# The first two tiles of an input projection in halves of the tokens

## The chip, the cores and the metric

The kernel runs on one core of one Trainium2 chip. The metric is the time of one execution in microseconds (us), measured on the device. The kernel before takes 2940.47 us, the median of three runs (2937.76 to 2942.84).

## The reference, cut to what matters

The reference is one hybrid decoder block over 512 tokens of 2048 channels in float32: an RWKV-7 time mixer and a sliding-window attention side by side, merged by sigmoid gates, then a gated feed-forward with a short convolution. What the change touches is its first step:

```python
h = rms_norm(x, norm1_g[l])      # per token: x * rsqrt(mean(x^2) + eps) * g
z = h @ w_in[l]                  # 2048 channels in, all branches' inputs out
...
q = za[..., :ATT_Q_DIM]
k = za[..., ATT_Q_DIM:ATT_Q_DIM + ATT_KV_DIM]
v = za[..., ATT_Q_DIM + ATT_KV_DIM:]
```

Each row (token) of `x` is scaled by a number of its own and each channel by its gain; the result is multiplied by the columns of `w_in`.

## The kernel before

**Products in three parts.** Every operand of a large product is split into a high part (the value rounded to the matmul format fp32r) and a low part (the rest). A product is three matmuls: high by high, high by low, low by high. Three such matmuls for one block of 128 channels are called one step here; a tile of 128 output columns takes 16 steps, 48 matmuls of 512 columns (the tokens), into one PSUM bank.

**The start.** `x` arrives in four tiles `xt[t]` of 128 tokens (line 171). ScalarE squares and sums each tile (L293), VectorE makes the reciprocal root of two tiles' sums in `rsqrt_small` (L188 to L197, thirteen small operations) and scales the two tiles (L296). That is done for the first two tiles (tokens 0 to 255, half `h=0`), then for the other two (`h=1`). Then, per half and per block `k` of 128 channels, TensorE transposes the two 128x128 pieces into a PSUM tile `ps_x` (L303), ScalarE writes the high part `xhi` with the gain (L305), and VectorE the low part `xlo` (L306). That is 2 x 16 columns, each 256 tokens wide, through six PSUM buffers.

**The weights.** `load_w` (L236) fetches four blocks of a tile's weights (256 KB) by a DMA on the queue of SyncE (SP) into one of four `raw` buffers, ScalarE writes the high part `whi` (L243), VectorE the low part `wlo` (L244), in three buffers each. `project` (L250) calls it four times a tile and issues the matmuls (L258 to L260). The first three loads of the first tile are written ahead of the columns, as `first`.

**The order of the tiles.** 72 tiles: the keys' first tile (`c_ka`), the values' first (`c_va`), further keys and values, queries, the RWKV inputs, the gates. `ztile` (L313) gives a tile an accumulator of the pool `accA` (three banks). Behind a tile of keys `qk_norm` takes sums of squares on TensorE (`head_stats`, L333) and turns them by a transpose (L336).

**Sums of weights in DRAM.** The later stages need sums of blocks of `w_out` and `w_down`. They are made in DRAM beside the projection: every third call of `load_w` (every fourth in the last 28 loads, `wp["step"] = 4`) starts one job, a DRAM to DRAM copy of 512 KB on SP (L227) and an accumulating DMA on GpSimd's queue (POOL, L228). Further jobs follow in the stages behind the projection. There are 120 in all.

**What sets the order.** The kernel is written in a framework that sets semaphores and orders each engine's instructions itself. An instruction passed through `pin` keeps its place relative to the other pinned instructions of its engine; the rest may be moved. Each engine works through its own list in order. In the projection before, the start and the loads of weights are not pinned.

**Towards the end of the projection** the outputs of the two branches are fetched from DRAM by DMAs on POOL's queue (`rin`, `ain`, L780 and L782), while the last gate tiles run.

Of the kernel before, what the change touches and what calls it, by code (L numbers as in the profile page):

```python
# [20 lines left out]
NT = S // P  # L21
# [5 lines left out]
RMS_EPS = 1e-6  # L27
# [107 lines left out]
def block_kernel(ctx: ExitStack, tc: tile.TileContext, d: Dims, a: dict, out: bass.AP):  # L135
    nc = tc.nc
    act, dve, pool, pe, sync = nc.scalar, nc.vector, nc.gpsimd, nc.tensor, nc.sync
    NK, NP, NQ, NKV, NF = d.NK, d.NP, d.NQ, d.NKV, d.NF
# [16 lines left out]
    ident = const.tile([P, P], F32, name="ident")  # L155
# [5 lines left out]
    cst = cstp.tile([P, NCONST - P], F32, name="cst")  # L161
# [18 lines left out]
    def col(nm, i=0):  # L180
        return pcol[:, PR[nm] + i : PR[nm] + i + 1]
# [51 lines left out]
        wp["raw"] = stack.enter_context(tc.tile_pool(name="wraw", bufs=nraw, side=side, reuse_waits="tile"))  # L233
        wp["hl"] = stack.enter_context(tc.tile_pool(name="whl", bufs=nhl, side=side, reuse_waits="tile"))

    def load_w(src):  # L236
        nk, ncol = src.shape[1:]
        n = nk * ncol
        raw = wp["raw"].tile([P, 512], F32, name="raw", tag="raw")[:, :n].rearrange("p (k c) -> p k c", c=ncol)
        wp["last"] = sync.dma_start(raw, src)  # L240
        hi = wp["hl"].tile([P, 512], F32R, name="whi", tag="whi")[:, :n].rearrange("p (k c) -> p k c", c=ncol)
        lo = wp["hl"].tile([P, 512], F32R, name="wlo", tag="wlo")[:, :n].rearrange("p (k c) -> p k c", c=ncol)
        act.activation(hi, raw, AF.Copy)  # L243
        dve.tensor_tensor(lo, raw, hi.bitcast(F32), op=ALU.subtract)  # L244
        wp["n"] += 1
        if wp["n"] % wp["step"] == 0:
            sums_along()()
        return hi, lo

    def project(acc, src, xhi, xlo, pre=()):  # L250
        nk = src.shape[1]
        for k0 in range(0, nk, 4):
            n = min(4, nk - k0)
            whi, wlo = pre[k0 // 4] if k0 // 4 < len(pre) else load_w(src[:, k0 : k0 + n])
            for j in range(n):
                k = k0 + j
                first, last = k == 0, k == nk - 1
                pe.matmul(acc, whi[:, j], xhi[:, k], start=first, stop=False)  # L258
                pe.matmul(acc, whi[:, j], xlo[:, k], start=False, stop=False)  # L259
                pe.matmul(acc, wlo[:, j], xhi[:, k], start=False, stop=last)  # L260
# [20 lines left out]
    pa = ExitStack()  # L281
    open_weights(pa, 4, 3, "right")
    if True:
        xhi = by_k(big(big1, "xhi", "h1"))
        xlo = by_k(big(big1, "xlo", "l1"))
        zt = {c: a["w_z"][i].rearrange("p (k c) -> p k c", c=P) for i, c in enumerate(d.z_tiles())}
        with tc.tile_pool(name="x0_ps", bufs=6, space=PSUM) as ps0:
            ssum = p0.tile([P, NT], F32, name="ssum")
            HT = NT // 2
            for h in range(2):  # L290
                for t in range(h * HT, (h + 1) * HT):
                    sq = p0.tile([P, d.D], F32, name="sqx", tag="sqx", bufs=1)
                    act.activation(sq, xt[t], AF.Square, accum_out=ssum[:, t : t + 1])  # L293
                r = rsqrt_small(p0, ssum[:, h * HT : (h + 1) * HT], 1.0 / d.D, RMS_EPS)
                for t in range(HT):
                    dve.tensor_scalar(xt[h * HT + t], xt[h * HT + t], r[:, t : t + 1], None, op0=ALU.mult)  # L296
            first = {d.c_ka: [load_w(zt[d.c_ka][:, k0 : k0 + 4]) for k0 in range(0, min(NK, 12), 4)]}
            for h in range(2):
                hs = slice(h * HT * P, (h + 1) * HT * P)
                for k in range(NK):  # L300
                    ps = ps0.tile([P, HT * P], F32, name="ps_x", tag="x")
                    for t in range(HT):
                        pe.transpose(ps[:, t * P : (t + 1) * P], xt[h * HT + t][:, k * P : (k + 1) * P], ident)  # L303
                    g = col("n1g", k)
                    act.activation(xhi[:, k, hs], ps, AF.Identity, scale=g)  # L305
                    dve.scalar_tensor_tensor(xlo[:, k, hs], ps, g, xhi[:, k, hs].bitcast(F32), op0=ALU.mult, op1=ALU.subtract)  # L306
        xin.close()
        act.activation(bor, K["bo"], AF.Copy)
        act.activation(cenr, K["cen"], AF.Copy)

        accp = pa.enter_context(tc.tile_pool(name="accA", bufs=3, space=PSUM, side="right", reuse_waits="tile"))
# [464 lines left out]
        with tc.tile_pool(name="ain", bufs=1, side="right", reuse_waits="tile") as ainp:  # L776
# [586 lines left out]
```

## Time and profile before

| | us |
|---|---|
| median of three runs | 2940.47 |
| lowest and highest | 2937.76, 2942.84 |
| the profiled execution, its own time | 2943.37 |
| its span in the trace | 2941.6 |
| TensorE busy | 2895.2 |
| VectorE busy | 1951.8 |
| ScalarE busy | 1315.9 |

The profile is one execution, 2.90 us above the median, and its span is 1.77 us short of its own time. PE is TensorE's matmul row, PEld its loading of the stationary operand (beside matmuls), DVE VectorE, ACT ScalarE, SPq the issuing of SyncE. A row of the timeline has start, duration, engine, line, operation, output and inputs, shapes, count (equal neighbours are merged), and in brackets the idle time before it and what ended that. A row of a table by windows has the window, its length, each engine's busy time with the number of instructions, the clock that was granted to TensorE (1.00 is full), the share of the 16 DMA engines and what they moved in GB/s. Matmuls overlap, so the distance between two starts is the price of one, not its duration.

### The profile page before, as it was taken

How to read it: one execution, taken by the hardware profiler on the slowest of the kernel's cores; microseconds unless marked ns; L12 is line 12 of the kernel's file. 1: busy time of each engine (PE TensorE's matmuls, PEld its weight loads, DVE VectorE, ACT ScalarE, POOL GpSimd, SP SyncE). 2: the span in 40 equal slices, each digit the busy share in tenths (PEclk: the TensorE clock that was granted, in tenths of full speed). 3: DMA queues.
4: the chain of work that ended last, by engine and by line, in shares of the span. 5: the costliest groups of instructions: out<-in, count | busy, mean ns of one | idle time of the engine just before them, and what ended most of it. 6: DMA issues, size and time to landing. Idle time of an engine off the chain costs nothing.

```text
span 2941.6 us, 48281 instructions
## 1 busy us (share of the span) xinstructions
PE 2895.2 (98%) x18826; PEld 2470.2 (84%) x18826; DVE 1951.8 (66%) x3243; ACT 1315.9 (45%) x2133; POOL 218.9 (7%) x286
## 2 busy tenths in 40 slices
PE   7999999999999999999999899999999999999999
PEld 5777777777777777788888899999999999888887
DVE  4555666666666666445567777777777777665555
ACT  4344434334334334332356455455555555544444
POOL 0001000000000000101000001101101110000000
PEclk9999999999999999999999899999999999999999
DMA  7855756656656656877877789888888888877775
GB/s 209 222 150 140 191 128 163 159 130 164 160 131 162 158 126 158 255 234 237 287 249 236 190 234 240 237 226 226 229 235 241 233 229 230 303 239 244 256 258 189
DMA packets 225141, 609.45 MB, mean 207 GB/s; under 512 B 24768, under 2 KB 44944, under 8 KB 223888
## 3 DMA queue, kind: packets, MB, share of 16 engines
q1 hardware_dynamic: 157504, 434.92, 46.6%
q0 software_dynamic: 36064, 132.14, 23.6%
q10 hardware_dynamic: 31344, 39.31, 3.9%
q8 instruction: 147, 2.41, 0.3%
q14 instruction: 82, 0.67, 0.1%
HBM read 556.62 MB, written 174.43 MB: 249 GB/s over the span
## 4 chain that ended last, share of the span: by engine, by line
PE 93%; DVE 2%; ACT 2%; DMA 1%; issue 1%; ACTq 0%; SPq 0%; DVEq 0%; POOLq 0%
PE X L1064 16%; PE acc L260 11%; PE acc L259 11%; PE X L931 11%; PE acc L258 11%; PE Y L931 8%; PE Y L1064 8%; PE Z L1064 4%; PE bulk L644 1%; PE mi L460 1%; PE psG L713 1%; PE bulk L706 1%; PE psS L724 1%; PE bulk L552 1%; PE bulk L683 1%
## 5 line engine op out<-in xcount | busy, mean ns | idle before, releaser
L260 PE MATMUL acc<-xhi,wlo 128*128 128x512 f32 x1152 | 472.2, 410 | 0.0
L258 PE MATMUL acc<-xhi,whi 128*128 128x512 f32 x1152 | 466.1, 405 | 1.9 <-DVE xlo L306 1.9
L259 PE MATMUL acc<-xlo,whi 128*128 128x512 f32 x1152 | 466.2, 405 | 0.0
L243 ACT ACTIVATE whi<-raw 128x512 fp32r<-128x512 f32 x352 | 220.4, 629 | 457.2 <-PE acc L259 372.4
L924 DVE TENSOR_TENSOR wlo<-raw,whi 128x1024 fp32r<-128x1024 f32 x210 | 257.0, 1224 | 207.9 <-ACT whi L923 207.9
L244 DVE TENSOR_TENSOR wlo<-raw,whi 128x512 fp32r<-128x512 f32 x352 | 240.5, 688 | 226.5 <-ACT whi L243 217.7
L923 ACT ACTIVATE whi<-raw 128x1024 fp32r<-128x1024 f32 x210 | 222.6, 1060 | 291.9 <-PE X L931 157.7
L1064 PE MATMUL X<-b,whi 128*128 128x256 f32 x1472 | 271.0, 285 | 2.3 <-DVE u L1084 0.9
L1064 PE MATMUL X<-t,whi 128*128 128x256 f32 x1408 | 260.4, 285 | 8.7 <-DVE u L1084 8.3
L1047 DVE TENSOR_TENSOR wlo<-raw,whi 128x1024 fp32r<-128x1024 f32 x176 | 214.9, 1222 | 78.4 <-ACT whi L1046 77.7
L1064 PE MATMUL Y<-t,whi 128*128 128x256 f32 x1408 | 257.6, 283 | 0.0
L260 PEld LDWEIGHTS acc<-xhi,wlo 128*128 128x128 f32 x1152 | 217.3, 189 | 43.8 <-issue 3.1
L259 PEld LDWEIGHTS acc<-xlo,whi 128*128 128x128 f32 x1152 | 217.4, 189 | 41.7 <-issue 2.2
L258 PEld LDWEIGHTS acc<-xhi,whi 128*128 128x128 f32 x1152 | 217.5, 189 | 41.4 <-issue 2.2
L1046 ACT ACTIVATE whi<-a 128x1024 fp32r<-128x1024 f32 x132 | 139.3, 1056 | 213.7 <-DVE a L1040 211.5
L1064 PEld LDWEIGHTS X<-b,whi 128*128 128x128 f32 x1472 | 231.2, 193 | 3.1 <-issue 2.4
L1064 PEld LDWEIGHTS X<-t,whi 128*128 128x128 f32 x1408 | 222.1, 194 | 9.3 <-DVE u L1084 5.7
L1064 PEld LDWEIGHTS Y<-t,whi 128*128 128x128 f32 x1408 | 220.2, 192 | 0.0
L1064 PE MATMUL X<-b,wlo 128*128 128x256 f32 x736 | 209.5, 285 | 2.1 <-DVE wlo L1047 2.1
L1047 DVE TENSOR_TENSOR wlo<-a,whi 128x1024 fp32r<-128x1024 f32 x132 | 161.7, 1225 | 67.6 <-ACT whi L1046 67.0
L1064 PE MATMUL X<-t,wlo 128*128 128x256 f32 x704 | 200.7, 285 | 0.2
L1064 PE MATMUL Y<-t,wlo 128*128 128x256 f32 x704 | 199.4, 283 | 0.0
(339 smaller groups left out, 6050.0 us busy)
## 6 DMA issues: line engine op xcount, KB each, us to landing
raw<-in_w_up_dram SPq DMA_DIRECT2D x180, 512.0 KB
raw<-in_w_z_dram SPq DMA_DIRECT2D x288, 256.0 KB
s_dn<-in_w_dn_dram POOLq DMA_DIRECT2D x88, 512.0 KB, 6.9
raw<-in_w_up_dram POOLq DMA_DIRECT2D x88, 512.0 KB, 8.3
raw<-s_dn SPq DMA_DIRECT2D x88, 512.0 KB
raw<-in_w_dn_dram SPq DMA_DIRECT2D x66, 512.0 KB
a<-in_w_up_dram SPq DMA_DIRECT2D x48, 512.0 KB
s_dn<-in_w_dn_dram SPq DMA_DIRECT2D x44, 512.0 KB
```

The source lines that it names most:

```text
L243: act.activation(hi, raw, AF.Copy)
L244: dve.tensor_tensor(lo, raw, hi.bitcast(F32), op=ALU.subtract)
L258: pe.matmul(acc, whi[:, j], xhi[:, k], start=first, stop=False)
L259: pe.matmul(acc, whi[:, j], xlo[:, k], start=False, stop=False)
L260: pe.matmul(acc, wlo[:, j], xhi[:, k], start=False, stop=last)
L460: pe.matmul(ps[:, h], pT[:, kb, h], vt[:, n - 1 + kb, g * HD : (g + 1) * HD], start=kb == kbs[0], stop=kb == kbs[-1])
L923: act.activation(whi, wr, AF.Copy)
L924: dve.tensor_tensor(wlo, wr, whi.bitcast(F32), op=ALU.subtract)
L931: pe.matmul(dst, l[:, q, ts], r[:, es], start=fst and j == 0, stop=lst and j == 2, skip_group_check=True)
L1046: pin(act.activation(hi, t, AF.Copy))
L1047: pin(dve.tensor_tensor(lo, t, hi.bitcast(F32), op=ALU.subtract))
L1064: pin(pe.matmul(ps, l[:, k], r[:, k], start=start and k + i == 0, stop=last and i == 2, skip_group_check=True))
```

## The change

The normalised rows are still made in two halves of 256 tokens, in this order now, almost all of it pinned:

- Squares of all four tiles; scale and scaling of the first half; its 16 columns (`columns(0, k)`). The second half's scale is written after the eighth column. After columns 9, 11, 13 and 15 stand the four loads of the first tile's weights, into buffers of their own in the pool of the rows (eight pairs for two tiles).
- Scaling of the second half: one tile on VectorE, one on ScalarE. The DMAs of the constants and of the attention sinks come here on SP instead of at the very start.
- The first tile's products with the first half of the tokens: 48 matmuls of 256 columns.
- For each `k`: at every fourth `k` a load of the second tile's weights; the column `k` of the second half; the second tile's three matmuls of block `k` with the first half.
- The second half of the tokens for the first tile, then for the second: 96 matmuls of 256 columns.

The accumulators of the two tiles are taken ahead of the columns' PSUM buffers, which are five now instead of six. The eight loads of these two tiles do not count towards the sums in DRAM, and the step of four for the last loads is gone, so that it stays three.

```diff
-    def load_w(src):
+    def load_w(src, pl=None, bufs=None, pin=free):
...
-        act.activation(hi, raw, AF.Copy)
-        dve.tensor_tensor(lo, raw, hi.bitcast(F32), op=ALU.subtract)
+        hi, lo = ((pl or wp["hl"]).tile([P, 512], F32R, name=nm, tag=nm, bufs=bufs)[:, :n].rearrange("p (k c) -> p k c", c=ncol)
+                  for nm in ("whi", "wlo"))
+        pin(act.activation(hi, raw, AF.Copy))
+        pin(dve.tensor_tensor(lo, raw, hi.bitcast(F32), op=ALU.subtract))
+        if pl:
+            return hi, lo
         wp["n"] += 1
         if wp["n"] % wp["step"] == 0:
             sums_along()()
...
-    sync.dma_start(sinkb, a["attn_sinks"].rearrange("(o h) -> o h", o=1).to_broadcast([P, d.HQ]))
-    sync.dma_start(cst, a["cst"][:, P:])
...
+        heads = [accp.tile([P, S], F32, name="acc", tag="acc") for _ in range(2)]
+        first = dict(zip((d.c_ka, d.c_va), heads))
+        with tc.tile_pool(name="x0_ps", bufs=5, space=PSUM) as ps0:
...
+            def scales(h):
+                return rsqrt_small(p0, ssum[:, h * HT : (h + 1) * HT], 1.0 / d.D, RMS_EPS)
+
+            def scaled(h, t, r, eng):
+                x = xt[h * HT + t]
+                if eng is dve:
+                    pin(dve.tensor_scalar(x, x, r[:, t : t + 1], None, op0=ALU.mult))
+                else:
+                    pin(act.activation(x, x, AF.Copy, scale=r[:, t : t + 1]))
+
+            def columns(h, k):
...
+                    pin(pe.transpose(ps[:, t * P : (t + 1) * P], xt[h * HT + t][:, k * P : (k + 1) * P], ident))
+                g = col("n1g", k)
+                pin(act.activation(xhi[:, k, hs], ps, AF.Identity, scale=g))
+                pin(dve.scalar_tensor_tensor(xlo[:, k, hs], ps, g, xhi[:, k, hs].bitcast(F32), op0=ALU.mult, op1=ALU.subtract))
+
+            def weights(i, k):
+                ws[i].append(load_w(zt[(d.c_ka, d.c_va)[i]][:, k : k + 4], p0, 2 * NK // 4, pin))
+
+            def half_mm(i, h, k):
+                hs = slice(h * HT * P, (h + 1) * HT * P)
+                whi, wlo = (w[:, k % 4] for w in ws[i][k // 4])
+                for j, (l, r) in enumerate(((whi, xhi), (whi, xlo), (wlo, xhi))):
+                    pin(pe.matmul(heads[i][:, hs], l, r[:, k, hs], start=h == 0 and k + j == 0,
+                                  stop=k == NK - 1 and j == 2, skip_group_check=True))
+
+            r = scales(0)
+            for t in range(HT):
+                scaled(0, t, r, dve)
+            ws = [[], []]
+            for k in range(NK):
+                columns(0, k)
+                if k == NK // 2 - 1:
+                    r = scales(1)
+                if k >= NK // 2 and k % 2:
+                    weights(0, 2 * (k - NK // 2 - 1))
+            for t in range(HT):
+                scaled(1, t, r, act if t else dve)
+            sync.dma_start(cst, a["cst"][:, P:])
+            sync.dma_start(sinkb, a["attn_sinks"].rearrange("(o h) -> o h", o=1).to_broadcast([P, d.HQ]))
+            for k in range(NK):
+                half_mm(0, 0, k)
+            for k in range(NK):
+                if k % 4 == 0:
+                    weights(1, k)
+                columns(1, k)
+                half_mm(1, 0, k)
+            for i in range(2):
                 for k in range(NK):
...
+                    half_mm(i, 1, k)
         xin.close()
-        act.activation(bor, K["bo"], AF.Copy)
-        act.activation(cenr, K["cen"], AF.Copy)
...
+        pin(act.activation(bor, K["bo"], AF.Copy))
+        pin(act.activation(cenr, K["cen"], AF.Copy))
 
         def ztile(c0):
+            if c0 in first:
+                return first.pop(c0)
             acc = accp.tile([P, S], F32, name="acc", tag="acc")
-            project(acc, zt[c0], xhi, xlo, first.pop(c0, ()))
+            project(acc, zt[c0], xhi, xlo)
             return acc
...
-            wp["step"] = 4
```

More of the change, by code (lines that the diff above doesn't have):

```diff
@@ L248, in load_w, with project @@
         return hi, lo
-    def project(acc, src, xhi, xlo, pre=()):
+    def project(acc, src, xhi, xlo):
         nk = src.shape[1]
@@ L253, in project @@
             n = min(4, nk - k0)
-            whi, wlo = pre[k0 // 4] if k0 // 4 < len(pre) else load_w(src[:, k0 : k0 + n])
+            whi, wlo = load_w(src[:, k0 : k0 + n])
             for j in range(n):
@@ L289, in block_kernel @@
             HT = NT // 2
[L290 to L294, printed above, removed]
-                for t in range(HT):
-                    dve.tensor_scalar(xt[h * HT + t], xt[h * HT + t], r[:, t : t + 1], None, op0=ALU.mult)
@@ L297, in block_kernel @@
-            first = {d.c_ka: [load_w(zt[d.c_ka][:, k0 : k0 + 4]) for k0 in range(0, min(NK, 12), 4)]}
-            for h in range(2):
-                hs = slice(h * HT * P, (h + 1) * HT * P)
-                for k in range(NK):
[L301 to L306, printed above, removed]
+            for t in range(NT):
+                sq = p0.tile([P, d.D], F32, name="sqx", tag="sqx", bufs=1)
+                act.activation(sq, xt[t], AF.Square, accum_out=ssum[:, t : t + 1])
```

6 lines of the change are left out of this document (2 added, 4 removed).

## The prediction

> **What bounds the kernel now.** The page first: one engine is busy nearly throughout, and the chain that ended last runs along it.
>
> ```profile
> span 2941.6 us, 48281 instructions
> PE 2895.2 (98%) x18826; PEld 2470.2 (84%) x18826; DVE 1951.8 (66%) x3243; ACT 1315.9 (45%) x2133; POOL 218.9 (7%) x286
> PE 93%; DVE 2%; ACT 2%; DMA 1%; issue 1%; ACTq 0%; SPq 0%; DVEq 0%; POOLq 0%
> ```
>
> So only two things can move the end: TensorE standing idle, or TensorE taking longer for the same products. The idle time is 46 us; the change can reach that part of it which lies ahead of the first product. The timeline of the first 60 us shows it:
>
> ```profile
> 13.72 2.48 DVE L296 TENSOR_SCALAR xi<-xi,rq 128x2048 f32<-128x2048 f32 x2
> 14.28 1.91 ACT L293 ACTIVATE sqx<-xi 128x2048 f32<-128x2048 f32 x1 [0.48 <-DMA xi<-in_x_dram]
> 16.80 0.16 DVE L193 TENSOR_SCALAR rq<-rq 128x2 f32<-128x2 f32 x1
> 17.27 0.48 DVE L306 SCALAR_TENSOR_TENSOR xlo<-ps_x,par,xhi 128x256 fp32r<-128x256 f32 x1 [0.32 <-ACT xhi L305]
> 17.74 0.48 DVE L306 SCALAR_TENSOR_TENSOR xlo<-ps_x,par,xhi 128x256 fp32r<-128x256 f32 x1
> 24.94 9.88 DVE L306 SCALAR_TENSOR_TENSOR xlo<-ps_x,par,xhi 128x256 fp32r<-128x256 f32 x25
> 25.47 7.49 PE L303 MATMUL ps_x<-ident,xi 128*128 128x128 f32 x38 [2.10 <-DVE xlo L306]
> 26.20 7.42 ACT L305 ACTIVATE xhi<-ps_x,par 128x256 fp32r<-128x256 f32 x19 [2.31 <-PE ps_x L303]
> 32.52 0.20 PEld L303 LDWEIGHTS ps_x<-ident,xi 128*128 128x128 f32 x2 [0.19 <-DVE xlo L306]
> 34.87 0.50 PE L258 MATMUL acc<-xhi,whi 128*128 128x512 f32 x1 [1.91 <-DVE xlo L306]
> 35.76 0.63 PE L258 MATMUL acc<-xhi,whi 128*128 128x512 f32 x1
> 37.04 0.63 PE L258 MATMUL acc<-xhi,whi 128*128 128x512 f32 x1
> ```
>
> VectorE sets the pace: from 17.27 it is busy without a gap, 0.395 us per `xlo` piece (9.88 / 25; a small operation between two adds 0.07, 17.27 to 17.74), ScalarE 0.39 per `xhi` (7.42 / 19). The first product starts at 34.87, when the 32nd piece is done. The first two tiles of the projection then take to 60.03:
>
> ```profile
> L258 PE MATMUL acc<-xhi,whi x32: 388/389/632, 34.9 to 59.4; 128*128 128x512 f32 x32
> 59.35 0.39 PE L258 MATMUL acc<-xhi,whi 128*128 128x512 f32 x1
> 60.03 0.39 PE L258 MATMUL acc<-xhi,whi 128*128 128x512 f32 x1
> 48.88 0.39 PE L258 MATMUL acc<-xhi,whi 128*128 128x512 f32 x1
> 50.07 0.47 PE L259 MATMUL acc<-xlo,whi 128*128 128x512 f32 x1
> 52.91 0.39 PE L259 MATMUL acc<-xlo,whi 128*128 128x512 f32 x1
> 53.57 0.48 PE L260 MATMUL acc<-xhi,wlo 128*128 128x512 f32 x1
> ```
>
> Two tiles hold 32 of these, so the one at 60.03 opens the third tile. Three products take 0.68, one 0.227. Head statistics interrupt twice: 50.07 - 48.88 - 0.23 = 0.96 and 53.57 - 52.91 - 0.23 = 0.43. They are paid after the change too, so the end to compare with is 60.03 - 1.39 = **58.64**. The granted clock by windows (the last three columns are clock, DMA share, GB/s):
>
> ```profile
> 18.53:21.95 3.42, 1.52 (x8) 0.63 (x7) 3.42 (x13) 3.42 (x10) 0.51 (x1) 0.99 0.72 242
> 25.36:28.77 3.41, 3.30 (x16) 3.10 (x17) 3.41 (x10) 2.57 (x7) 0.00 (x0) 0.51 0.99 226
> 28.77:32.19 3.42, 3.42 (x21) 1.89 (x20) 3.42 (x10) 3.42 (x11) 0.82 (x1) 1.00 0.11 32
> 35.56:38.97 3.41, 3.41 (x10) 2.66 (x9) 0.00 (x0) 0.00 (x0) 0.00 (x0) 0.50 0.02 5
> ```
>
> A stretch with TensorE busy 1.52 of 3.42 us is followed by half clock; one full of transposes (25.36 to 28.77) by full clock. The first products after the pause ran at half for 3.41 us, a loss of 1.7.
>
> **The change, stage one: columns of the first half.** VectorE starts at 17.27 as before. It now does 16 `xlo` (6.32), the low parts of the first tile's four weight loads, the small operations of the second scale (thirteen, the fourth of them at 16.80; nine behind 17.27, 0.6), and one scaling (2.48 / 2 = 1.24). Prices of a weight load:
>
> ```profile
> 39.29 0.63 ACT L243 ACTIVATE whi<-raw 128x512 fp32r<-128x512 f32 x1 [5.67 <-PE acc L259]
> 39.95 0.69 DVE L244 TENSOR_TENSOR wlo<-raw,whi 128x512 fp32r<-128x512 f32 x1 [5.13 <-ACT whi L243]
> ```
>
> 17.27 + 6.32 + 0.6 + 4 x 0.69 + 1.24 = 28.2 for the scaled rows of the second half; ScalarE, which scales the other tile (as long as a square, 1.91), is free earlier. TensorE's own order is fixed: all 16 pairs of transposes, then the 48 half products of tile one. With five PSUM buffers the 16th pair waits for the 11th `xlo`: 17.27 + 11 x 0.395 + 0.6 + 0.69 = 22.9, so the products start at 23.2. A 256-column product costs, from the up projection:
>
> ```profile
> 2000.00:2050.00 50.00, 50.00 (x419) 50.00 (x418) 1.00 0.82 220
> ```
>
> 50 / 419 = 0.119. 48 of them end at 28.95, their weights just ahead of them (the last low part at 26.95). If a half-clock window falls here it costs up to 1.7; I take half of that: **29.85**. The halves as such cost 192 x 0.119 - 96 x 0.227 = 1.1 in all, contained in these sums.
>
> **Stage two: second columns between products of tile two.** By VectorE alone this would be 16 x 0.395 + 3 x 0.69 = 8.4 us. But all three engines are pinned to program order, and TensorE does transposes k, products k, transposes k+1. At each fourth k the products wait for a new low part; that stands on VectorE behind its high part, which stands on ScalarE behind the `xhi` of the column before, which needs a pair of transposes that stands on TensorE behind the previous group's products. The loop closes: three column steps of products (3 x 0.358), two pairs of transposes before the third (2 x 0.20, from 32.52), from the start of that pair to its `xhi` 0.6, `xhi` 0.39, high part to low part 0.66, low part 0.69, release 0.05 = **3.86 per group of four** where VectorE's own work is 2.27. The 0.6 is the last pair at 32.52 against the last `xhi`:
>
> ```profile
> L305 ACT ACTIVATE xhi<-ps_x,par x32: 467/488/561, 16.8 to 33.1; 128x256 fp32r<-128x256 f32 x32
> ```
>
> First group 4.06 (one pair more), two at 3.86, the last 4 x 0.358 + 3 x 0.20 = 2.03: 13.8. Then the second halves of both tiles, 96 x 0.119 = 11.45. End: 29.85 + 13.8 + 11.45 = 55.1, so **3.5 earlier** than 58.64. What is late next there: the third tile's weights, but VectorE and ScalarE have nothing else for the last 11 us, so nothing. The constants (801 KB) and the sinks, moved on SP behind four weight loads, are wanted only after the columns, and DMA stands nearly idle at 28.77 to 32.19 (share 0.11). The attention tiles that take the place of the rows are first written after tile one; if they waited for tile two as well, statistics would come 5.7 late behind a third tile that runs anyway: 0.
>
> **The late stage.** The eight loads of the first two tiles no longer count towards the DRAM sums, and the last 28 loads of the projection issue one every third load instead of every fourth. The number is unchanged (86 + 7 = 93 = 280 / 3), the places are not. Most of the way the phase of the sums only shifts, and weights are early; not so near 1235, where the rows of the mixed branches are fetched. ScalarE, SP and TensorE there:
>
> ```profile
> 1226.90 0.63 ACT L243 ACTIVATE whi<-raw 128x512 fp32r<-128x512 f32 x1 [3.74 <-DMA raw<-in_w_z_dram]
> 1231.27 0.63 ACT L243 ACTIVATE whi<-raw 128x512 fp32r<-128x512 f32 x1 [3.74 <-DMA raw<-in_w_z_dram]
> 1235.47 0.63 ACT L243 ACTIVATE whi<-raw 128x512 fp32r<-128x512 f32 x1 [3.57 <-DMA raw<-in_w_z_dram]
> 1213.46 0.50 SPq L227 DMA_DIRECT2D s_dn<-s_dn  x1
> 1218.48 0.33 SPq L240 DMA_DIRECT2D raw<-in_w_z_dram  x1
> 1221.20 3.05 SPq L240 DMA_DIRECT2D raw<-in_w_z_dram  x2
> 1224.60 0.49 SPq L227 DMA_DIRECT2D s_dn<-s_dn  x1
> 1216.00:1236.00 20.00, 20.00 (x90) 16.51 (x88) 3.48 (x6) 4.17 (x7) 5.12 (x8) 1.00 1.02 376
> 1236.16 0.49 PE L258 MATMUL acc<-xhi,whi 128*128 128x512 f32 x1
> ```
>
> Loads land 4.2 to 4.4 apart while TensorE eats one in 2.72, DMA is full (1.02), and the high part of load 279 (issued 1221.20) is ready at 1236.1 as TensorE needs it (1236.16): no margin is left. Before, sums stood behind loads 276, 280 and 284; after, behind 275, 278 and 281. One copy more, 512 KB, is ahead of load 279. Bounds: 0, if the order on SP shifts; 8.7, two loads at 4.37. A DRAM copy moves some 209 GB/s when DMA is full:
>
> ```profile
> 1171.00:1172.00 1.00, 1.00 (x7) 0.87 (x6) 0.20 (x1) 0.00 (x0) 0.00 (x0) 1.00 1.05 209
> ```
>
> 512 KB at that is an estimated **2.5**, which I take: with the DMA engines full it is their work in all that puts the end off, and the bounds' nearer end is the small one. The Trainium skill (DMA: Bandwidth & Descriptors, Queues, rings and completion order) says that a DMA engine takes turns between the queues that have work, packet by packet; while POOL's fetches run, the copy would cost SP's queue twice its own time, an estimated 5.0, and the sum would be +1.5. The spacing of the loads agrees with such sharing.
>
> Sum: -3.5 + 2.5 = -1.0. The profiled execution took 2943.37 (span 2941.6 and 1.77 around it), 2.90 above the median 2940.47; the difference carries over: 2942.4 for such an execution, **2939.5** as a median.
>
> **Rivals.** (A) Stage two keeps VectorE's pace: the first low part of a group comes early enough. Then the last low part is done 0.6 + 0.5 + 12 x 0.395 + 3 x 0.69 = 7.9 behind the first pair, the stage takes 7.9 + 2.03 = 9.9 and the gain is 7.4: 2935.6 with the late copy, 2933.1 without. For it: idle VectorE in the loop; against: the pinned orders. (B) The burst at 1235 isn't lengthened: 2937.0. For it: the sums' places depend on the order that the planner gives SP. (C) Slower: the clock. If transposes between products don't hold it, TensorE enters the first half products cold (1.7 instead of the 0.8 taken), and in stage two its products fill 5.7 of 13.8 us, 41%, near the 1.52 of 3.42 that was followed by half clock. At half clock three products take 0.64 (half of 37.04 - 35.76), a pair 0.37 (2 x 3.10 / 17), start to `xhi` 0.73 (25.47 to 26.20): groups 5.55, 5.18, 5.18, 3.67 = 19.6, 5.8 more; the next products lose 1.7. With 0.8 that is 8.3 on the forecast: 2947.8. [...] Against it: 28.77 to 32.19, pairs of transposes alone, kept the full clock. The Trainium skill (TensorE: Matmul & The Clock Gate, Part 4: PE-mode transpose) states that the full clock doesn't engage for transposes; the trace disagrees, since the clock rose at 28.77 (0.51 to 1.00) after a window that held only transposes. (D) The burst pays the full 8.7: 2945.7.
>
> **How the numbers follow.** A measurement of this kernel can tell about 0.2%, 5.9 us, from no change. Forecast 0.45, A 0.18, B 0.15, C 0.12, D 0.10. Faster by over that (under 2934.6): most of A and the edge of B, 0.15. Slower (over 2946.4): C and half of D, 0.15. Else 0.70. The range leaves out C and the best of A: 2933 to 2946.
>
> **What would show it.** First half product near 23, 12 us earlier than now; three waits of TensorE for a low part in stage two, 1.6 us each, with VectorE idle between; third tile at 55 to 56.5, statistics included; clock 0.5 at most once before 30; a wait of TensorE of 2 to 3 us for weights near 1230, which is not there now. Wrong would be: no waits in stage two (A), half clock in 30 to 44 (C), or a stage after 60 that moved by more than 3 us.

## The result, and the profile after

The kernel after takes 2953.58 us, the median of five runs (2948.16 to 2956.40), beside 2937.80 for the kernel before, run beside it (2937.60 to 2942.84, five runs). The ratio is 1.0042, with a 95% interval from 1.0030 to 1.0053: slower by 0.42%, about 12 us, where 1 us less was forecast. The profiled execution of after took 2948.16, 5.4 below its median; its page:

```profile
span 2946.4 us, 48467 instructions
PE 2897.7 (98%) x18922; PEld 2473.2 (84%) x18922; DVE 1949.0 (66%) x3242; ACT 1316.0 (45%) x2134; POOL 219.4 (7%) x286
PE 92%; DVE 3%; ACT 2%; DMA 2%; issue 1%; ACTq 0%; SPq 0%; DVEq 0%
```

The shares are those of before. A page of averages can't show a change of 0.4%, so the same instruction was looked up in both traces, and the distance between its two starts taken (after minus before; negative is earlier). The evictions of the gate tiles serve as marks: `gt<-acc`, 32 of them, each behind the last product of its tile. Of before, the third, 23rd, 27th and 32nd:

```profile
444.83 0.58 ACT L327 ACTIVATE gt<-acc 128x512 f32<-128x512 f32 x1
1138.94 0.58 ACT L327 ACTIVATE gt<-acc 128x512 f32<-128x512 f32 x1
1209.47 0.58 ACT L327 ACTIVATE gt<-acc 128x512 f32<-128x512 f32 x1
1264.33 0.60 ACT L327 ACTIVATE gt<-acc 128x512 f32<-128x512 f32 x1 [7.75 <-PE acc L260]
```

The same four of after:

```profile
440.21 0.58 ACT L372 ACTIVATE gt<-acc 128x512 f32<-128x512 f32 x1
1142.41 0.58 ACT L372 ACTIVATE gt<-acc 128x512 f32<-128x512 f32 x1
1213.61 0.58 ACT L372 ACTIVATE gt<-acc 128x512 f32<-128x512 f32 x1
1274.97 0.60 ACT L372 ACTIVATE gt<-acc 128x512 f32<-128x512 f32 x1 [7.59 <-PE acc L262]
```

The distances are -4.6, +3.5, +4.1 and +10.6. So there is a **gain of 4.6** at the start (already there at the first gate, -4.65), a **loss of 8.1** between 445 and 1139, where the RWKV pairs are computed, and a **loss of 6.5** between 1209 and 1264, where the branch outputs are fetched. The loss in the pairs comes in one step of 1.0 right behind 445 and then six of 1.1 to 1.3, one for each pair. The first step is a wait, which the kernel before does not have: TensorE stands for a low part of weights, and VectorE makes it late, behind rows that a DMA brought late. In after:

```profile
443.82 0.69 DVE L799 TENSOR_TENSOR yc<-yc,rsb 128x512 f32<-128x512 f32 x1 [5.50 <-DMA rsb<-rsd]
446.47 0.50 PE L262 MATMUL acc<-xhi,wlo 128*128 128x512 f32 x1 [0.71 <-DVE wlo L244]
```

The six others show no such wait.

Behind 1264 the profiled pair gives back 5.9, 10.6 down to 4.8 at the end. Before's profiled execution had TensorE at a lower clock in places where after's had not, for instance (before, then after; the clock is the third column from the right):

```profile
2510.00:2530.00 20.00, 17.83 (x89) 14.95 (x88) 16.03 (x22) 11.07 (x15) 2.13 (x4) 0.91 0.95 352
```

```profile
2515.00:2535.00 20.00, 19.34 (x113) 16.78 (x112) 18.07 (x26) 11.08 (x14) 2.14 (x4) 1.00 0.88 303
```

Whether the change has a part in this was not shown. Against the same trace of before, phase_back of the table below gives back 0.5 there, start_alone 3.3 and phase_alone 6.8, so that traces differ by this much. Up to 1264 the steps add up to +10.6, near the 12 that the ratio gives.

**The start.** These rows of TensorE answer to the forecast's stages one and two, and the last one is the second tile's eviction:

```profile
24.24 0.56 PE L325 MATMUL acc<-xhi,whi 128*128 128x256 f32 x1
26.31 0.29 PE L325 MATMUL acc<-xhi,whi 128*128 128x256 f32 x1
30.91 0.38 PE L313 MATMUL ps_x<-ident,xi 128*128 128x128 f32 x2
34.11 0.38 PE L325 MATMUL acc<-xhi,whi 128*128 128x256 f32 x1 [0.50 <-ACT whi L243]
36.93 0.47 PE L260 MATMUL acc<-xhi,whi 128*128 128x512 f32 x1
42.38 0.39 PE L325 MATMUL acc<-xhi,whi 128*128 128x256 f32 x1 [0.93 <-ACT whi L243]
45.23 0.28 PE L325 MATMUL acc<-xhi,whi 128*128 128x256 f32 x1
56.43 0.40 PE L261 MATMUL acc<-xlo,whi 128*128 128x512 f32 x1
56.62 0.60 ACT L437 ACTIVATE vf<-acc 128x512 f32<-128x512 f32 x1 [10.68 <-PE acc L325]
```

The first half products start at 24.24, stage two runs from 30.91 to 45.23, the second halves to 56.43. At 36.93 TensorE does something the forecast did not have: a product of the third tile (512 columns). The framework put ten of these into stage two, so at 56.43 the third tile is ten products, 2.27 us, ahead.

### The profile page after: what moved, and what is told of

It reads as the page before. It is cut to its first block, busy times and chain, and to the rows that moved or that the text cites. A ratio compares the mean times of both kernels' runs of the same rounds, so it can differ in the third digit from the quotient of the medians.

```text
span 2946.4 us, 48467 instructions
## 1 busy us (share of the span) xinstructions
PE 2897.7 (98%) x18922; PEld 2473.2 (84%) x18922; DVE 1949.0 (66%) x3242; ACT 1316.0 (45%) x2134; POOL 219.4 (7%) x286
## 4 chain that ended last, share of the span: by engine, by line
PE 92%; DVE 3%; ACT 2%; DMA 2%; issue 1%; ACTq 0%; SPq 0%; DVEq 0%
PE X L1108 17%; PE X L975 11%; PE acc L262 10%; PE acc L261 10%; PE acc L260 10%; PE Y L975 8%; PE Y L1108 8%; PE Z L1108 4%; PE psG L758 1%; PE bulk L689 1%; PE mi L505 1%; PE bulk L751 1%; PE psS L769 1%; PE bulk L728 1%; DMA raw<-in_w_z_dram 1%
## 5 line engine op out<-in xcount | busy, mean ns | idle before, releaser
L262 PE MATMUL acc<-xhi,wlo 128*128 128x512 f32 x1120 | 460.0, 411 | 0.7 <-DVE wlo L244 0.7
L260 PE MATMUL acc<-xhi,whi 128*128 128x512 f32 x1120 | 454.9, 406 | 4.0 <-ACT whi L243 4.0
L261 PE MATMUL acc<-xlo,whi 128*128 128x512 f32 x1120 | 453.9, 405 | 0.0
L262 PEld LDWEIGHTS acc<-xhi,wlo 128*128 128x128 f32 x1120 | 211.3, 189 | 44.2 <-issue 3.1
L260 PEld LDWEIGHTS acc<-xhi,whi 128*128 128x128 f32 x1120 | 211.6, 189 | 43.2 <-ACT whi L243 5.2
L261 PEld LDWEIGHTS acc<-xlo,whi 128*128 128x128 f32 x1120 | 211.3, 189 | 40.3 <-issue 3.1
L1091 DVE TENSOR_TENSOR wlo<-a,whi 128x1024 fp32r<-128x1024 f32 x132 | 161.7, 1226 | 68.2 <-ACT whi L1090 67.6
```

What stands on the lines that cost most here:

```text
L1091: pin(dve.tensor_tensor(lo, t, hi.bitcast(F32), op=ALU.subtract))
```

## The experiments

All are read by the same marks. The table has the step between neighbouring marks against the kernel before, so that a cause can be placed: "start" is the distance at the first gate (243.8), then the steps to the third (444.8), the 23rd (1138.9), the 27th (1209.5) and the 32nd (1264.3). The last columns are the median and the ratio with its interval.

```
kernel           start  to 445  pairs  to 1209  burst   median    ratio
after             -4.7    0.0   +8.1    +0.7    +6.5   2953.58   1.0042 [1.0030, 1.0053]
start_alone       -2.6   -0.1   -0.3    +0.3    -0.3   2937.25   0.9993 [0.9984, 1.0002]
sums_alone        -0.5   +4.8   +7.2    +0.1    +6.9   2957.47   1.0056 [1.0044, 1.0069]
phase_back        -0.7   -0.3   -0.3    +0.3    +6.7   2944.55   1.0017 [1.0009, 1.0026]
phase_alone       -0.5   +3.7   +7.0    +0.5    +6.1   2954.84   1.0053 [1.0040, 1.0066]
phase_third       -1.7   +2.8   +0.5     0.0    -0.2   2942.46   1.0012 [1.0003, 1.0021]
phase_less_add    -0.7   -1.5   +7.0    +0.5    +3.7   2948.56   1.0031 [1.0020, 1.0043]
rate_back         -4.4   +4.1   +6.6    +0.7    +4.3   2951.43   1.0046 [1.0032, 1.0060]
start_ahead       -4.7   -0.3   -0.3     0.0    -0.4   2936.25   0.9988 [0.9980, 0.9997]
quiet_end         -4.5   +2.8   +8.0    +0.6    +0.2   2966.30   1.0086 [1.0072, 1.0100]
before_empty      -0.3   -1.4   -0.3    +0.1    +0.4   not compared
after_empty       -6.0   -1.4   +6.9    +0.7    +0.8   not compared
```

**Which half of the change costs.** The change has two parts: the start itself, and the sums in DRAM, which the start moves because its eight loads no longer count and the step of four is gone. start_alone is the kernel after with both undone:

```diff
-        if pl:
-            return hi, lo
         wp["n"] += 1
...
+            wp["step"] = 4
             for i in range(4):
                 emit_gate()
```

> The changed kernel with the old places of the sums: the eight loads of the first two tiles count again, and the last 28 loads step by four. Theory 'places': the loss lies in the places of the sums alone, so what is left is the start's own gain, 4.6 us as the changed kernel's trace has it behind the second tile: about 2933, no steps of 1.1 per pair, no extra wait near 1235. Rival 'start': the new start shifts what follows it by itself; then the seven steps of 1.1 remain and the time stays near 2945 or above.

sums_alone is the kernel before with only the sums moved as in after:

```diff
-    wp = {"n": 0, "step": 3}
+    wp = {"n": -8, "step": 3}
...
-        if wp["n"] % wp["step"] == 0:
+        if wp["n"] > 0 and wp["n"] % wp["step"] == 0:
...
-            wp["step"] = 4
```

> The kernel before with the new places of the sums: its first eight loads don't count, and the step stays three to the end. Theory 'places': all that was lost comes with it, 7 x 1.1 in the pairs and 6.9 at the burst: 2937.8 + 14.8, about 2952. Rival 'start': within 2 us of before.

The start alone has neither loss (-0.3 in the pairs, -0.3 in the burst), the sums alone have both (+7.2, +6.9). The moved sums make the kernel slower; the start is a gain in the traces. As a median it can't be told from nothing: 2937.25 beside 2939.50 for the kernel before in those runs, where 2933 was expected. The median of sums_alone lies 5 above the 2952 expected; its trace has a further +4.8 ahead of 445, which is taken up below. The size of the start's gain hangs on the sums too: -2.6 in start_alone, with sums among the first eight loads again, and TensorE's last wait for weights in stage two is 2.95 long where after has the 0.93 above.

**Which part of the moved sums.** With eight loads uncounted, a sum stands behind loads 11, 14, 17 and so on of the old count, where the kernel before has it behind 9, 12, 15: one load earlier, seen modulo three. The missing step of four adds sums behind load 260. phase_back is after with the old places, but step three to the end:

```diff
-    wp = {"n": 0, "step": 3}
+    wp = {"n": 8, "step": 3}
```

> The changed kernel whose count of loads starts at eight, so that the sums in the pairs stand at the loads where they stood before; the step of three at the end stays. Theory 'places': the pairs lose nothing, the burst still does: 2937.8 - 4.6 + 0 to 7, that is 2933 to 2940, by the copy that stands ahead of the loads in need. Rival 'start': the steps of 1.1 remain, 2945 or above.

phase_alone and phase_third are the kernel before with the step of four kept and the places shifted by one load (as after has them) and by two (a 2 in place of the 1):

```diff
-    wp = {"n": 0, "step": 3}
+    wp = {"n": 1, "step": 3}
```

> The kernel before with its count of loads started at one: every sum one load earlier, step of four at the end as before. Theory 'places': the pairs lose 7 x 1.1, the burst nothing much: about 2945.6, with steps of 1.1 per pair in the trace. Rival 'rate': the loss hangs on the number of sums per load, not on their places; then within 2 us of before.

> The kernel before with its count of loads started at two: every sum two loads earlier. TensorE's order is the same as before, the sums' transfers fall elsewhere. Theory 'order': the pairs lose nothing, the time is within 2 us of before apart from the burst near 1235. Rival 'traffic': the pairs move by 0.5 us each or more, one way or the other.

The pairs lose with one shift (phase_alone, +7.0), not with the old places (phase_back, -0.3) and not with the other shift (phase_third, +0.5). The burst was to be a matter of the step alone; it isn't: it costs +6.7 with the step of three and the old places, +6.1 with the step of four and the shift. That expectation of phase_alone failed, and so did that of rate_back, the kernel after with the sums beside the last 28 loads put back to the very loads of before:

```diff
+            wp["step"] = 4
             for i in range(4):
                 emit_gate()
...
-    wp["step"] = 12
+    wp["step"] = 9
```

> The changed kernel with the step of four back for the last 28 loads (and every ninth load instead of every twelfth in the stage behind, so that all sums are made). Theory 'places': the burst of 6.9 shrinks to 2 or less, the pairs still lose 7 x 1.1: 2937.8 - 4.6 + 7.8 + 0 to 2, about 2941 to 2943. If the burst's loss hangs on the exact load and not on the rate, it stays near 2948 to 2950.

The pairs keep their loss, as expected, but the burst keeps +4.3 of its 6.5. The list of sums is not that of before, though. SyncE issues the first eight loads of the next stage inside the projection, four of them in the burst. With the eight loads of the start uncounted, the last of these brings the count to 288, a multiple of the next stage's step (twelve in after, nine here), so that a copy stands behind it. The kernel before, whose count is eight further on, has none until the twelfth load, at 1276.8. In the burst rate_back issues copies at 1220.38, 1226.33 and 1232.93 (behind load 276 of the projection, behind that eighth load, behind load 280), before at 1213.46 and 1224.60 (behind 276 and 280). So rate_back does not tell what the other thing that differs costs, that it comes to the burst 6.9 us late.

**Why the pairs lose.** Two theories. Order: with the sums moved, the framework, which arranges each engine's instructions itself, writes another order of TensorE's instructions in the pairs, and that order is worse by itself. Place: the sums now meet the loads of the pairs at a bad moment. For the first spoke that every kernel with the loss has one and the same new order of TensorE there, and every kernel without it the old one; but these also have the sums in the one place that loses. phase_less_add is phase_alone with the accumulating DMAs cut to an eighth of the columns, so that it leaves seven eighths of each second summand out:

```diff
-        return lambda: pool.dma_start(dst, quarter(w, second, c)[q], accum_op=ALU.add, ...)
+        return lambda: pool.dma_start(dst[:, :DH // 8], quarter(w, second, c)[q][:, :DH // 8], accum_op=ALU.add, ...)
```

> As phase_alone, with every engine's order the same, but the accumulating DMA of each sum moves an eighth of its columns (seven eighths of each second summand are left out of the sums). Theory 'order': the pairs lose because each engine's instructions stand in another order there, so the loss of phase_alone (7 x 1.1) remains. Rival 'traffic': the pairs lose because the sums' transfers now meet the round trips of the statistics through DRAM; with most of the accumulating traffic gone the pairs lose less than half.

The loss stays (+7.0); the copies, though, were whole. Three kernels were to part order from place, by having POOL issue the copies: there the order in the pairs is the old one wherever the sums stand. One is the kernel before with only that, one has the shift by one as well, one is the kernel after with it.

```diff
-        pin(sync.dma_start(dst, quarter(w, first, c)[q], max_dma_last_dim=4096))
+        pool.dma_start(dst, quarter(w, first, c)[q], max_dma_last_dim=4096)
```

> The kernel before, with the copy of each sum issued by GpSimd (POOL) ahead of its accumulating DMA, instead of by SyncE: same sums beside the same loads, and the order of TensorE's and ScalarE's instructions is that of the kernel before. It is the base line of the next run. Both theories of the loss in the RWKV pairs (the order of the instructions; the places of the sums) expect no step there: the distance of the same gate eviction from the kernel before changes by less than 1 us between 445 and 1139 us. What the other queue costs by itself shows at the end: about 2939 us, 2936 to 2943.

> As the run before it, with the count of loads begun at 1, so that every sum stands one load earlier, as in phase_alone. With the copies on POOL the order of all instructions of TensorE, VectorE and ScalarE is the same as in the run before it, where phase_alone had another order in the pairs. Theory order: the pairs lose nothing, the step between 445 and 1139 us is 0 (below 1 us), and the kernel takes 2939 to 2946 us (the burst near 1235 us can still cost up to 6). Theory place (the sums get in the way of the pairs' loads one load earlier): the step is +7 as in phase_alone (+7.0), the kernel 2946 to 2955 us.

> The kernel after, with the copies issued by POOL. The sums stand where those of the kernel after stand, step of three to the end included, but the order of TensorE's and ScalarE's instructions in the pairs is that of the kernel before. Theory order: start -4 to -5, pairs 0, burst 0 to +7, so 2935 to 2943 us, which is 10 below the kernel after (2953.6). Theory place: pairs +7 to +8, so 2943 to 2951 us.

They missed by 120 us and more, and tell nothing of the question. They took 3083.94, 3078.90 and 3072.61 us (ratios 1.0491 [1.0477, 1.0506], 1.0465 [1.0444, 1.0486] and 1.0452 [1.0438, 1.0467]). On SP a copy stands behind a load that waits for a free buffer, and that wait is what spreads the sums over the projection; on POOL nothing held them. The share of the DMA engines, in 40 slices, of the first of the three:

```profile
DMA  9999999953322332355677777877777877877775
```

All 240 transfers were issued by 650 us, where the kernel before has about 15 in every 100 us up to 1300. Most pairs ran without sums and in the old order, and from 478 us to 1139 the distance stays within 0.4 in all three, as either theory would have it.

before_empty and after_empty do it the other way round: the bytes go, TensorE's two orders stay. Beside the projection only an eighth of each sum is copied and added; all sums are made whole behind it, which costs some 365 us there (3306.96 and 3308.45 us, one run each), so that only the part before 1264 is read.

```diff
+        if wp["step"] < 12:
+            made.append((w, (n, first, second), c, q))
+            d8 = slice(0, DH // 8)
+            pin(sync.dma_start(dst[:, d8], quarter(w, first, c)[q][:, d8], ...))
+            return lambda: pool.dma_start(dst[:, d8], quarter(w, second, c)[q][:, d8], accum_op=ALU.add, ...)
...
     wp["step"] = 12
+    rest, jobs[:] = list(jobs), made
+    while jobs:
+        sums_along()()
+    jobs[:] = rest
```

> The kernel before, with every sum beside the projection cut to an eighth of its columns, copy and accumulating DMA both; the full sums are made in one go behind the projection, which costs hundreds of us there (about 93 MB in each direction), so the end is not read. TensorE's and ScalarE's order up to there is that of the kernel before. It is the base line of the next run. Both theories expect no step against the kernel before between 445 and 1139 us (below 1 us), and none in the burst from 1209 to 1264 us or a gain of 1 to 3.

> The kernel after, changed in the same way: an eighth of each sum beside the projection, the rest behind it. TensorE's order in the pairs is that of the kernel after. Distance of the same instruction from the run before it: behind the start -4 to -5 in both theories. Theory order (the pairs lose because the new order splits pairs of small products): it grows by 7 to 8 between 445 and 1139 us, although only an eighth of the bytes is moved. Theory transfers (the sums meet the pairs' loads at the wrong moment): it grows by less than 1.5. Burst from 1209 to 1264 us: less than 1.5 more, if the sums are what it loses to (as quiet_end says), 4 to 7 if not. The end is not read.

The pairs' stretch of both, between the same two gates, rounded to the us (PE's busy time is the second figure):

```profile
443.00:1137.00 694.00, 691.52 (x4902) 524.41 (x4901) 463.96 (x1018) 285.84 (x577) 45.56 (x58) 1.00 0.35 85
```

```profile
437.00:1138.00 701.00, 697.59 (x4902) 526.71 (x4901) 463.62 (x1018) 284.28 (x576) 45.56 (x58) 1.00 0.35 84
```

The same 4902 products, the DMA engines at 0.35 in both, and 7 us more. Of these 6.07 are "busy" time of TensorE. From before_empty to after_empty the distance grows by 6.9 - (-0.3) = 7.2 in the pairs, with an eighth of the bytes: **the order is the cause** of the six steps, the transfers are not. The first step of after, the wait at 446, is gone with the bytes (0.0 in after_empty): this 1.0 of the 8.1 belongs to the transfers. With the bytes whole the windows of before and after read much the same:

```profile
445.00:1139.00 694.00, 691.49 (x4900) 524.13 (x4899) 464.61 (x1018) 285.47 (x576) 45.55 (x58) 1.00 0.62 152
```

```profile
441.00:1142.00 701.00, 696.71 (x4896) 525.66 (x4896) 463.23 (x1018) 283.28 (x574) 45.76 (x58) 1.00 0.61 151
```

What differs in the order can be seen in one link of the chain of small products that runs through a pair (`psG`, 64 columns). Before, TensorE's rows; x4 is two neighbouring pieces of the link:

```profile
528.48 0.34 PE L713 MATMUL psG<-SV,AB 128*64 128x64 f32 x4
528.74 0.50 PE L258 MATMUL acc<-xhi,whi 128*128 128x512 f32 x1
529.08 0.40 PE L259 MATMUL acc<-xlo,whi 128*128 128x512 f32 x1
529.32 0.39 PE L260 MATMUL acc<-xhi,wlo 128*128 128x512 f32 x1
```

After, the same link of the same pair:

```profile
525.35 0.33 PE L758 MATMUL psG<-SV,AB 128*64 128x64 f32 x2
525.61 0.50 PE L262 MATMUL acc<-xhi,wlo 128*128 128x512 f32 x1
526.04 0.33 PE L758 MATMUL psG<-SV,AB 128*64 128x64 f32 x2
526.30 0.51 PE L260 MATMUL acc<-xhi,whi 128*128 128x512 f32 x1
526.64 0.40 PE L261 MATMUL acc<-xlo,whi 128*128 128x512 f32 x1
```

A large product has been put between the two pieces. Four small and two large products take 529.32 - 528.48 = 0.84 before and 526.64 - 525.35 = 1.29 after, 0.45 more: two pieces cost 0.26 whether alone or together, and a large product alone between small ones takes 0.43, where in a row it takes 0.23 to 0.24. The pair at 520 to 540 has two such splits more than before. Over all pairs, by the distances between starts of neighbouring matmuls:

```
                     before (445 to 1139)     after (440.4 to 1142.3)
large to large       1487, 369.3 us           1475, 367.3 us
large to small        334,  97.6 us            346, 104.7 us
small to small       2742, 198.1 us           2730, 199.3 us
small to large        334,  28.4 us            346,  30.3 us
```

Twelve more changes each way, two for each of the six steps, and 7.1 us more in the second row. Every kernel of the table with the loss has 346 changes and 104.3 to 104.7 us in that row, every one without it 334 and about 97.6. The idle time of TensorE shows little of this (0.9 of the 7 us between the two windows with few bytes), since the matmuls' modelled durations cover the gaps. Twelve splits at 0.45 are 5.4. A further 1.0 are six waits of under 0.2, one in each step, for a small operation of VectorE (`rq`, L197), which before does not have (nor does rate_back, whose loss is 6.6). The last 0.7 was not followed. ScalarE's order changes together with TensorE's; TensorE's waits for ScalarE in the pairs are the same in both (1.8 in all).

**Why the burst loses.** The theory was the sums; the rival, that the new order or the later fetches do it. quiet_end is the kernel after without any sum beside the last 28 loads:

```diff
+            wp["step"] = 1000
             for i in range(4):
                 emit_gate()
...
-    wp["step"] = 12
+    wp["step"] = 4
```

> The kernel after without any sum beside the last 28 loads of the projection (the nine left over are made in the next stage, every fourth load there instead of every twelfth). The order of TensorE's instructions is that of the kernel after. Theory sums (the burst loses because copies of 512 KB meet the fetches of the branch outputs): the step between 1209 and 1264 us falls from +6.7 to 0 or below, the pairs keep their +7, and the kernel takes about 2947 us, if the next stage hides the nine. Theory order or fetches (the burst loses without the sums): the step stays at +4 to +7, about 2952 us.

The burst's step is +0.2 in place of +6.5, with the order of TensorE of after; in after_empty it is +0.8, beside +0.4 in before_empty. So it is the sums' bytes. quiet_end is not quite without them: with its step of four a copy still stands behind the eighth load of the next stage, at 1223.8, inside the burst. That one copy, with the others gone, costs nothing that the step shows. TensorE's waits near the burst, of after and of quiet_end (total, times, longest):

```profile
PE acc L260 <- ACT whi L243: 4.0, 2, 2.5
```

```profile
PE acc L260 <- ACT whi L243: 0.4, 1, 0.4
```

quiet_end as a whole is slower still, 2966.30: the sums moved on cost 22 in the next stage (the distance from after goes from -3.5 at 1288 to +18.6 at 1468), and TensorE's waits for high parts of weights total 14.1 us in it, for the 4.0 of after. The expected 2947 missed for that.

**A version that keeps the gain.** start_ahead is start_alone with the second tile's four loads written ahead of the first tile's half products:

```diff
+            for k in range(0, NK, 4):
+                weights(1, k)
             for k in range(NK):
                 half_mm(0, 0, k)
             for k in range(NK):
-                if k % 4 == 0:
-                    weights(1, k)
                 columns(1, k)
```

> As start_alone, with all four weight loads of the second tile ahead of the first half products, so that the loop through the low parts in stage two is gone. If the loop is what stage two loses by, TensorE does stage two in about 16 x 0.57 = 9.1 us without waits for weights, and the third tile starts 1.5 to 3 us earlier than in start_alone: 2930 to 2932. If the planner's filling with the third tile's products had covered the loop's waits, it is within 1 us of start_alone.

It has the whole gain of the start (-4.7) and no loss behind it, and it is the one kernel here that beats the kernel before, by 0.12% (interval 0.03% to 0.20%). Its median, 2936.25, missed the 2930 to 2932 expected; the third tile's lead on start_alone, 2.1 us at the first gate, is as expected.

## Why the prediction was wrong

**Stage one** was right but for a microsecond: first half product at 24.24 (forecast 23.2), second stage at 30.91 (forecast 29.85), half clock for its first part, one window, as the clock shows:

```profile
22.90:26.30 3.40, 3.09 (x14) 2.69 (x14) 3.40 (x8) 3.03 (x6) 0.00 (x0) 0.50 0.41 87
26.30:29.70 3.40, 3.40 (x30) 3.40 (x30) 3.11 (x5) 1.74 (x2) 0.00 (x0) 1.00 0.65 202
```

**Stage two** was right in kind: 14.3 us, forecast 13.8, with waits for weights, not rival A's 9.9. Sixteen columns at 0.57 are 9.1, so 5.2 is lost, near the forecast's three waits of 1.6. But 2.27 of it is filled with the third tile's products, which the forecast did not think of; they stand in the second and third wait, and what is left of the third is 0.93. The first has no filling; it is 0.50 for the high part and 0.23 for the low. That is the missing microsecond: counted like the forecast, 56.43 less the 2.27 done ahead is 54.2 where 55.1 was said, and the gain is 4.5 by that count (4.65 at the first gate) for 3.5. Rival C did not happen; with transposes between products the clock was 1.00 from 30.9 to 45.2.

**The step that failed** is in "The late stage": "Most of the way the phase of the sums only shifts, and weights are early." The sentence took the order of the instructions as given. The shift changes that order, and this costs 7.1 us (7.2 with the bytes taken away), which the forecast priced at nothing and gave no rival. With it the sum would have been -1.0 + 7.1 = +6.1, or 2946.6, outside the range. Weights are early there, but not everywhere: the wait at 446 costs another 1.0. The forecast had named the sign of this itself, a stage behind 60 that moves by more than 3 us.

**The burst** was in the right place and of the right kind, but mis-sized: +6.5 for the 2.5 taken, inside the bounds of 0 to 8.7. The step that failed there is "One copy more, 512 KB, is ahead of load 279". Two more are. SyncE in after:

```profile
1215.99 0.50 SPq L227 DMA_DIRECT2D s_dn<-s_dn  x1
1217.78 3.70 SPq L240 DMA_DIRECT2D raw<-in_w_b_dram  x4
1221.57 0.47 SPq L240 DMA_DIRECT2D raw<-in_w_z_dram  x1
1222.13 0.49 SPq L227 DMA_DIRECT2D s_dn<-s_dn  x1
1224.37 0.33 SPq L240 DMA_DIRECT2D raw<-in_w_z_dram  x1
1225.66 0.47 SPq L227 DMA_DIRECT2D s_dn<-s_dn  x1
1228.95 9.62 SPq L240 DMA_DIRECT2D raw<-in_w_z_dram  x3
```

The copies stand behind load 275, behind the eighth load of the next stage (the last of the four `in_w_b` loads here) and behind 278; the last row begins with 279. The kernel before has one from 1213 up to its load 279, behind 276 (1213.46). The forecast did not see that the uncounted loads also bring forward a sum of the next stage. Two copies at its 2.5 are 5.0.

The way in which they cost time is not the forecast's, though. The load that comes late first is 277, issued at 1221.57, ahead of two of the three copies. ScalarE waits 8.20 for it, and TensorE stands; it stands again for load 279:

```profile
1236.85 0.63 ACT L243 ACTIVATE whi<-raw 128x512 fp32r<-128x512 f32 x1 [8.20 <-DMA raw<-in_w_z_dram]
1241.57 0.63 ACT L243 ACTIVATE whi<-raw 128x512 fp32r<-128x512 f32 x1 [4.09 <-DMA raw<-in_w_z_dram]
1246.38 0.63 ACT L243 ACTIVATE whi<-raw 128x512 fp32r<-128x512 f32 x1 [4.18 <-DMA raw<-in_w_z_dram]
1237.54 0.50 PE L260 MATMUL acc<-xhi,whi 128*128 128x512 f32 x1 [2.52 <-ACT whi L243]
1247.07 0.50 PE L260 MATMUL acc<-xhi,whi 128*128 128x512 f32 x1 [1.48 <-ACT whi L243]
1238.00:1241.50 3.50, 3.50 (x10) 2.56 (x9) 0.21 (x1) 0.00 (x0) 0.00 (x0) 0.51 1.06 346
```

The two waits are 4.0 us, and behind the first the clock is at half for about 3.4 us, which costs 1.7 more: 5.7 of the 6.5. The forecast had work for all engines and no clock.

The price of a copy is not settled by this. The row at 1171.00, from which the 2.5 was worked out, shows POOL's accumulating DMA alone. The copy issued at 1162.23 moved 184 GB/s at a DMA share of 0.80 (1163 to 1165), an estimated 2.3 us for 512 KB at a full share, so by luck the misreading changes little. The Trainium skill (DMA: Bandwidth & Descriptors, Queues, rings and completion order) was cited there for turns between queues, packet by packet, by which one copy would cost an estimated 5.0. The trace of before agrees with the turns: between 1226 and 1236, with the engines full, POOL's queue and SP's moved 638 packets each. The measured 6.5 lies between two copies at 2.5 and two at 5.0.

**What stays open.** Between 330 and 367 us, sums_alone, phase_alone, phase_third, rate_back and quiet_end lose 2.8 to 4.8, and the profiled execution of after doesn't, though up to there rate_back and quiet_end issue what it issues. Here are rate_back and after, in that order:

```profile
340.00:350.00 10.00, 7.49 (x25) 5.60 (x25) 8.26 (x18) 3.00 (x6) 1.01 (x2) 0.83 0.73 185
```

```profile
340.00:350.00 10.00, 8.61 (x45) 6.59 (x43) 9.69 (x24) 5.56 (x13) 0.81 (x1) 1.00 0.79 200
```

TensorE is busy for 1.1 us less there, and the mean clock is 0.83. The loss is not there in before_empty, after_empty and phase_less_add, which move fewer bytes, and neither in before, start_alone and phase_back, which move them all. It probably happens in most executions of after as well, which would account for some of the 5.4 by which the profiled one lies below the median; that was not shown.

Which of the copies make the burst longer is open too. phase_back and phase_alone lose 6.7 and 6.1 without a copy behind the eighth load of the next stage, and phase_third, with copies behind 274, 278 and 282, loses nothing. How copies that are issued behind load 277 make it late was not found.

## What to carry to other kernels

In a kernel whose order is arranged by a framework, moving a DMA can change the order of other engines' instructions hundreds of microseconds away: compare the order of the instructions first, and only then the transfers. A busy engine is no measure of progress; the distance between the same instruction in two traces is, and it shows in a few rows where time went. When a change carries a second one with it (here the count that paces other work), take the first alone: the whole loss was in the second.

## What the runs showed of the hardware

- A 512-column product takes 0.23 to 0.24 us in a row of its kind and 0.43 alone between 64-column products; two groups of the small ones take 0.26 together and 0.26 each when split.
- A stall of TensorE of 2.5 us within the burst was followed by half clock for about 3.4 us, so a short stall cost 1.7 more than itself. The Trainium skill (TensorE: Matmul & The Clock Gate, What's actually happening) has the clock follow windows of about 3.4 us of activity; the length of the half-clock stretches here, 3.4 both times (22.9 to 26.3 and 1238.1 to 1241.5), agrees.
- With the DMA engines full, the queues of POOL and SP moved equal numbers of packets (638 each in before, 1226 to 1236), though not equal bytes (2.40 and 1.25 MB).
- Copies and accumulating DMAs from DRAM to DRAM that nothing held back took the DMA engines' share to nine tenths for the first 600 us and slowed the kernel by 145 us (pool_copy_base). Spread over 1300 us by the waits of SP's queue, seven eighths of their bytes cost 1.5 us up to 1264 (before against before_empty).
